# Huber loss on one core: subtraction in pieces, one load queue, a fourth output buffer, and a hand-ordered end

## The chip, the cores and the metric

The kernel runs on one core of a Trainium2 chip. The metric is device time in microseconds (us), the median of the executions. All runs told here were in the fast state, every kernel gave the right result, and the TensorE clock plays no part, as TensorE does nothing. Engine names in the profile: POOL is GpSimd, DVE is VectorE, ACT is ScalarE, SP is SyncE (it only issues loads here); a small q after a name (ACTq) is that engine's instruction sequencer.

## The reference

Two inputs of 8192 x 8192 in fp32, one output of the same shape in fp32:

```python
diff = pred - target
abs_diff = np.abs(diff)
return np.where(abs_diff <= 1.0, 0.5 * diff**2, abs_diff - 0.5)
```

That is 537 MB in, 268 MB out, and a handful of elementwise operations on 67 million elements. The kernel computes it as 0.5 * min(|d|, 1)^2 + max(|d| - 1, 0).

## The kernel before

The array is cut into 64 row tiles of 128 x 8192. Each tile is loaded in two halves of 4096 columns, each half as a pair of 2.10 MB loads. The differences are kept in bf16; the store converts back to fp32 on its way out.

```python
pool_a = ctx.enter_context(tc.tile_pool(name="sbuf_a", bufs=3))
pool_b = ctx.enter_context(tc.tile_pool(name="sbuf_b", bufs=3))
pool_d = ctx.enter_context(tc.tile_pool(name="sbuf_d", bufs=2))
pool_s = ctx.enter_context(tc.tile_pool(name="sbuf_s", bufs=3))
# ... emit_loads(i), for each half j of tile i:
nc.sync.dma_start(out=a, in_=pred_t[i, :, c0 : c0 + COLS])
beng = nc.sync if j == 0 else nc.scalar          # second halves on ScalarE's queue
beng.dma_start(out=b, in_=targ_t[i, :, c0 : c0 + COLS])
# ... do_tail, for the tile before:
nc.scalar.activation(out=s, in_=s, func=Act.Square, scale=SQRT_HALF)   # L68
nc.scalar.activation(out=d, in_=d, func=Act.Relu, bias=neg1.ap())      # L69
nc.vector.tensor_tensor(out=s, in0=s, in1=d, op=Alu.add)               # L70
# ... the loop:
for i in range(n_rt):
    emit_loads(i + 1)
    do_tail(0)
    for j in range(n_ct):
        nc.gpsimd.tensor_tensor(                                       # L85
            out=dfull[:, c0 : c0 + COLS], in0=a, in1=b, op=Alu.subtract)
    nc.scalar.activation(out=dfull, in_=dfull, func=Act.Abs)           # L90
    nc.vector.tensor_scalar(                                           # L91
        out=sfull, in0=dfull, scalar1=1.0, scalar2=None, op0=Alu.min)
    flush(1)                  # the store of an earlier tile, issued by GpSimd (L63)
    pending_tail.append((sfull, dfull, i))
```

A scheduler orders the instructions of each engine, so the order of the source is not always the order that runs.

Of the kernel before, what the change touches and what calls it, by code (L numbers as in the profile page):

```python
# [1 line left out]

# [4 lines left out]


@with_exitstack
def kernel(  # L10
    ctx: ExitStack,
    tc: tile.TileContext,
    pred: bass.AP,
    target: bass.AP,
    out: bass.AP,
):
    nc = tc.nc
    P = 128
    fp32 = mybir.dt.float32
    bf16 = mybir.dt.bfloat16  # L20
    Alu = mybir.AluOpType
    Act = mybir.ActivationFunctionType

    n_rows, n_cols = pred.shape
    COLS = 4096
    n_ct = n_cols // COLS
    SQRT_HALF = 0.70710678118654752

    pred_t = pred.rearrange("(n p) m -> n p m", p=P)
    targ_t = target.rearrange("(n p) m -> n p m", p=P)  # L30
    out_t = out.rearrange("(n p) m -> n p m", p=P)
    n_rt = pred_t.shape[0]

    neg1 = nc.alloc_sbuf_tensor("huber_neg1_bf16", [P, 1], bf16)
    nc.gpsimd.memset(neg1.ap(), -1.0)  # L35

    pool_a = ctx.enter_context(tc.tile_pool(name="sbuf_a", bufs=3))
    pool_b = ctx.enter_context(tc.tile_pool(name="sbuf_b", bufs=3))
    pool_d = ctx.enter_context(tc.tile_pool(name="sbuf_d", bufs=2))
    pool_s = ctx.enter_context(tc.tile_pool(name="sbuf_s", bufs=3))  # L40

    loads = {}
    pending_tail = []
    pending_store = []

    def emit_loads(i):
        if i >= n_rt:
            return
        tl = []
        for j in range(n_ct):  # L50
            c0 = j * COLS
            a = pool_a.tile([P, COLS], fp32)
            b = pool_b.tile([P, COLS], fp32)
            nc.sync.dma_start(out=a, in_=pred_t[i, :, c0 : c0 + COLS])  # L54
            beng = nc.sync if j == 0 else nc.scalar
            beng.dma_start(out=b, in_=targ_t[i, :, c0 : c0 + COLS])  # L56
            tl.append((a, b))
        loads[i] = tl

    def flush(limit):  # L60
        while len(pending_store) > limit:
            r, pi = pending_store.pop(0)
            nc.gpsimd.dma_start(out=out_t[pi, :, :], in_=r)  # L63

    def do_tail(limit):
        while len(pending_tail) > limit:
            s, d, pi = pending_tail.pop(0)
            nc.scalar.activation(out=s, in_=s, func=Act.Square, scale=SQRT_HALF)  # L68
            nc.scalar.activation(out=d, in_=d, func=Act.Relu, bias=neg1.ap())  # L69
            nc.vector.tensor_tensor(out=s, in0=s, in1=d, op=Alu.add)  # L70
            pending_store.append((s, pi))

    emit_loads(0)
    for i in range(n_rt):
        dfull = pool_d.tile([P, n_cols], bf16)
        sfull = pool_s.tile([P, n_cols], bf16)

        emit_loads(i + 1)

        do_tail(0)  # L80

        for j in range(n_ct):
            c0 = j * COLS
            a, b = loads[i][j]
            nc.gpsimd.tensor_tensor(  # L85
                out=dfull[:, c0 : c0 + COLS], in0=a, in1=b, op=Alu.subtract
            )
        del loads[i]

        nc.scalar.activation(out=dfull, in_=dfull, func=Act.Abs)  # L90
        nc.vector.tensor_scalar(  # L91
            out=sfull, in0=dfull, scalar1=1.0, scalar2=None, op0=Alu.min,
        )

        flush(1)

        pending_tail.append((sfull, dfull, i))

    do_tail(0)
    flush(0)  # L100


# [1 line left out]
_INS = ['pred', 'target']  # L104
_OUTS = [((8192, 8192), 'float32')]


# [23 lines left out]
```

## Time and profile before

| | before |
|---|---|
| median of four runs | 1942.36 us (1942.27 to 1942.46) |
| span of the profiled run | 1940.8 us |
| bytes moved | 805.4 MB, 415 GB/s on average |
| one tile in the steady part | 29.63 us |

The costliest groups of the page of the kernel before. Columns: line, engine, operation, output and input, shapes, count; then the busy us and the mean ns of one; then the idle us just before them and what ended most of it.

```profile
L85 POOL TENSOR_TENSOR dfull<-a,b 128x4096 bf16<-128x4096 f32 x128 | 1253.1, 9804 | 607.1 <-issue 577.8
L68 ACT ACTIVATE sfull<-sfull 128x8192 bf16<-128x8192 bf16 x64 | 449.9, 7030 | 543.9 <-DVE sfull L91 543.9
L70 DVE TENSOR_TENSOR sfull<-sfull,dfull 128x8192 bf16<-128x8192 bf16 x64 | 283.2, 4426 | 903.0 <-ACT dfull L69 903.0
L91 DVE TENSOR_SCALAR sfull<-dfull 128x8192 bf16<-128x8192 bf16 x64 | 539.6, 8432 | 199.9 <-ACT dfull L90 199.9
```

To see: the min (L91) costs more than the add (L70), though it reads one input instead of two, and ScalarE's Square (L68) loses 543.9 us waiting for it. GpSimd's idle time is put down to "issue", so no wait that the profile shows ended it; the prediction works out from the timeline what it really waits for.

### The profile page before, as it was taken

What the parts mean: (1) busy time and instruction counts of PE and PEld (TensorE: products, weight loads), DVE (VectorE), ACT (ScalarE), POOL (GpSimd) and SP (SyncE); (2) the same over time, 40 slices, a digit from 0 to 9 for tenths busy, and PEclk for the clock granted to TensorE, in tenths of its full rate; (3) what the DMA queues carried; (4) which work ended last, traced back from release to release, by engine and by line L of the source; (5) the groups of instructions that cost most, each with busy time, mean ns of one, the idle gap of its engine ahead of it and who ended that gap; (6) DMA issues with size and microseconds to landing.
All of it is one profiled execution on the core that took longest, in us unless ns stands there. A gap on an engine that the chain in (4) does not pass through costs nothing.

```text
span 1940.8 us, 1386 instructions
## 1 busy us (share of the span) xinstructions
DVE 822.9 (42%) x128; ACT 1343.0 (69%) x193; POOL 1286.6 (66%) x197
## 2 busy tenths in 40 slices
DVE  0345344354353453443543534534434435345342
ACT  2866867767668668677677686686676776866865
POOL 5676676676766766866767667668667676676680
DMA  9999999999999999999999999999999999999966
GB/s 404 376 420 428 421 427 426 425 424 424 424 428 422 426 424 424 425 425 423 426 426 423 427 424 424 422 429 423 424 425 426 425 424 424 424 424 424 426 274 260
DMA packets 46091, 805.42 MB, mean 415 GB/s; under 512 B 5120, under 2 KB 5120, under 8 KB 5120
## 3 DMA queue, kind: packets, MB, share of 16 engines
q1 hardware_dynamic: 27648, 402.67, 53.5%
q0 software_dynamic: 9216, 268.44, 32.5%
q10 hardware_dynamic: 9216, 134.22, 16.2%
q14 instruction: 11, 0.09, 0.0%
HBM read 536.87 MB, written 268.44 MB: 415 GB/s over the span
## 4 chain that ended last, share of the span: by engine, by line
ACT 50%; DVE 27%; issue 20%; POOL 1%; DMA 1%; POOLq 0%; SPq 0%; ACTq 0%
DVE sfull L91 27%; ACT dfull L90 22%; ACT sfull L68 22%; ACT dfull L69 6%; POOL dfull L85 1%; DMA b<-in_target_dram 1%; POOL out_dram L63 0%; POOLq L126 0%; SPq L54 0%; ACTq L56 0%; POOLq L85 0%; POOLq L63 0%
## 5 line engine op out<-in xcount | busy, mean ns | idle before, releaser
L85 POOL TENSOR_TENSOR dfull<-a,b 128x4096 bf16<-128x4096 f32 x128 | 1253.1, 9804 | 607.1 <-issue 577.8
L68 ACT ACTIVATE sfull<-sfull 128x8192 bf16<-128x8192 bf16 x64 | 449.9, 7030 | 543.9 <-DVE sfull L91 543.9
L70 DVE TENSOR_TENSOR sfull<-sfull,dfull 128x8192 bf16<-128x8192 bf16 x64 | 283.2, 4426 | 903.0 <-ACT dfull L69 903.0
L91 DVE TENSOR_SCALAR sfull<-dfull 128x8192 bf16<-128x8192 bf16 x64 | 539.6, 8432 | 199.9 <-ACT dfull L90 199.9
L90 ACT ACTIVATE dfull<-dfull 128x8192 bf16<-128x8192 bf16 x64 | 448.8, 7013 | 33.2 <-POOL dfull L85 33.2
L69 ACT ACTIVATE dfull<-dfull,huber_neg_bf 128x8192 bf16<-128x8192 bf16 x64 | 454.8, 7106 | 0.0
L63 POOL DMA_DIRECT2D out_dram<-sfull x64 | 36.6, 572 | 32.4 <-DVE sfull L70 32.4
L90 ACT ACT_TABLE_LOAD x1 | 1.3, 1283 | 1.2 <-PEq L115 1.2
L35 POOL MEMSET huber_neg_bf<- 128x1 bf16 x1 | 0.1, 101 | 0.3 <-POOLq L115 0.3
L115 POOL MEMSET const-float32-0.0<- 128x1 f32 x1 | 0.1, 98 | 0.2 <-issue 0.2
L115 POOL MEMSET const-bfloat16-1.0<- 128x1 bf16 x1 | 0.1, 101 | 0.0
L115 POOL MEMSET const-uint8-127<- 128x1 uint8 x1 | 0.1, 101 | 0.0
L115 POOL MEMSET const-float32-1.0<- 128x1 f32 x1 | 0.1, 98 | 0.0
## 6 DMA issues: line engine op xcount, KB each, us to landing
a<-in_pred_dram SPq DMA_DIRECT2D x128, 2048.0 KB, 18.0
out_dram<-sfull POOLq DMA_DIRECT2D x64, 4096.0 KB, 20.0
b<-in_target_dram ACTq DMA_DIRECT2D x64, 2048.0 KB, 13.8
b<-in_target_dram SPq DMA_DIRECT2D x64, 2048.0 KB, 24.6
```

What stands on the lines that cost most here:

```text
L35: nc.gpsimd.memset(neg1.ap(), -1.0)
L63: nc.gpsimd.dma_start(out=out_t[pi, :, :], in_=r)
L68: nc.scalar.activation(out=s, in_=s, func=Act.Square, scale=SQRT_HALF)
L69: nc.scalar.activation(out=d, in_=d, func=Act.Relu, bias=neg1.ap())
L70: nc.vector.tensor_tensor(out=s, in0=s, in1=d, op=Alu.add)
L85: nc.gpsimd.tensor_tensor(out=dfull[:, c0 : c0 + COLS], in0=a, in1=b, op=Alu.subtract)
L90: nc.scalar.activation(out=dfull, in_=dfull, func=Act.Abs)
L91: nc.vector.tensor_scalar(out=sfull, in0=dfull, scalar1=1.0, scalar2=None, op0=Alu.min,)
L115: nc = _bacc.Bacc("TRN2", target_bir_lowering=False, num_devices=1)
```

## The change

The intent is to let VectorE's min get in between shorter subtractions, to keep the loads in one queue that never runs dry, and to draw the last two tiles apart so that they do not pass the whole chain one after the other. There are four parts: four output buffers instead of three; all target loads on the sync queue; each half subtracted in two pieces of 2048 columns, with GpSimd's order fixed by hand; and the last two tiles written out by hand in small pieces, VectorE taking part of the work of ScalarE and GpSimd.

```diff
-    pool_s = ctx.enter_context(tc.tile_pool(name="sbuf_s", bufs=3))
+    pool_s = ctx.enter_context(tc.tile_pool(name="sbuf_s", bufs=4))
-            beng = nc.sync if j == 0 else nc.scalar
+            beng = nc.sync
-    for i in range(n_rt):
+    with tc.manual_schedule(engines={mybir.EngineType.Pool}):
+        for i in range(n_rt - 2):
 ... (loads, tail and the rest of the body as before)
-            nc.gpsimd.tensor_tensor(
-                out=dfull[:, c0 : c0 + COLS], in0=a, in1=b, op=Alu.subtract
-            )
+                for h0 in range(0, COLS, COLS // 2):
+                    h1 = h0 + COLS // 2
+                    nc.gpsimd.tensor_tensor(
+                        out=dfull[:, c0 + h0 : c0 + h1],
+                        in0=a[:, h0:h1], in1=b[:, h0:h1], op=Alu.subtract)
 ... (the end; orders of POOL, DVE and ACT fixed by hand)
+    flush(2)  # the store of tile 59
+    with tc.manual_schedule(engines=order):
+        asq(s61); arelu(d61)                    # tile 61's tail
+        ...                                     # tile 62: two subtractions on GpSimd
+        flush(1)  # the store of tile 60
+        vclamp(s_h1, d_h1); vstt(s_h1, d_h1); vmul(s_h1, d_h1)   # 62, half 1: VectorE alone
+        st62h1()
+        vadd(s61, d61)
+        flush(0)  # the store of tile 61
+        aabs(d_h0); vmin(s_h0, d_h0); asq(s_h0); arelu(d_h0)     # 62, half 0
+        sub63(V, 0); sub63(V, 1); sub63(V, 2)                    # 63: subtracted by VectorE
+        vadd(s_h0, d_h0); st62h0()
+        sub63(V, 3)
+        ... # 63: quarters 0 and 2 by Abs/min/Square/Relu/add, 1 and 3 by VectorE alone;
+        ... # four stores of one quarter each
```

(Several statements are put on one line here, and small helpers are left out: vclamp, vstt and vmul compute c = clamp(d, -1, 1), then c * (d - c/2), which is the same function without ScalarE.)

More of the change, by code (lines that the diff above doesn't have):

```diff
@@ L71, in do_tail, with act_path @@
             pending_store.append((s, pi))
-    emit_loads(0)
-    for i in range(n_rt):
-        dfull = pool_d.tile([P, n_cols], bf16)
-        sfull = pool_s.tile([P, n_cols], bf16)
-        emit_loads(i + 1)
-        do_tail(0)
+    def act_path(d, s):
+        nc.scalar.activation(out=d, in_=d, func=Act.Abs)
+        nc.vector.tensor_scalar(
+            out=s, in0=d, scalar1=1.0, scalar2=None, op0=Alu.min
+        )
+        nc.scalar.activation(out=s, in_=s, func=Act.Square, scale=SQRT_HALF)
+        nc.scalar.activation(out=d, in_=d, func=Act.Relu, bias=neg1.ap())
+        nc.vector.tensor_tensor(out=s, in0=s, in1=d, op=Alu.add)
@@ new lines, in dve_path @@
+    def dve_path(d, s):
+        nc.vector.tensor_scalar(
+            out=s, in0=d, scalar1=-1.0, scalar2=1.0, op0=Alu.max, op1=Alu.min
+        )
+        nc.vector.scalar_tensor_tensor(
+            out=d, in0=s, scalar=-0.5, in1=d, op0=Alu.mult, op1=Alu.add
+        )
+        nc.vector.tensor_tensor(out=s, in0=s, in1=d, op=Alu.mult)
+    emit_loads(0)
+    with tc.manual_schedule(engines={mybir.EngineType.Pool}):
+        for i in range(n_rt - 2):
+            dfull = pool_d.tile([P, n_cols], bf16)
+            sfull = pool_s.tile([P, n_cols], bf16)
+            emit_loads(i + 1)
+            do_tail(0)
+            for j in range(n_ct):
+                c0 = j * COLS
+                a, b = loads[i][j]
+                for h0 in range(0, COLS, COLS // 2):
+                    h1 = h0 + COLS // 2
+                    nc.gpsimd.tensor_tensor(
+                        out=dfull[:, c0 + h0 : c0 + h1],
+                        in0=a[:, h0:h1],
+                        in1=b[:, h0:h1],
+                        op=Alu.subtract,
+                    )
+            del loads[i]
+            nc.scalar.activation(out=dfull, in_=dfull, func=Act.Abs)
+            nc.vector.tensor_scalar(
+                out=sfull, in0=dfull, scalar1=1.0, scalar2=None, op0=Alu.min,
+            )
+            flush(1)
+            pending_tail.append((sfull, dfull, i))
@@ new lines, with vmin, vclamp @@
+    i62 = n_rt - 2
+    i63 = n_rt - 1
+    H = n_cols // 2
+    d62 = pool_d.tile([P, n_cols], bf16, tag="dfull")
+    s62 = pool_s.tile([P, n_cols], bf16, tag="sfull")
+    emit_loads(i63)
+    (s61, d61, _i61) = pending_tail.pop(0)
+    pending_store.append((s61, _i61))
+    V, A, G = nc.vector, nc.scalar, nc.gpsimd
+    def vmin(s, d):
+        V.tensor_scalar(out=s, in0=d, scalar1=1.0, scalar2=None, op0=Alu.min)
+    def vclamp(s, d):
+        V.tensor_scalar(
+            out=s, in0=d, scalar1=-1.0, scalar2=1.0, op0=Alu.max, op1=Alu.min
+        )
@@ new lines, in vstt, with vmul, vadd, aabs @@
+    def vstt(s, d):
+        V.scalar_tensor_tensor(
+            out=d, in0=s, scalar=-0.5, in1=d, op0=Alu.mult, op1=Alu.add
+        )
+    def vmul(s, d):
+        V.tensor_tensor(out=s, in0=s, in1=d, op=Alu.mult)
+    def vadd(s, d):
+        V.tensor_tensor(out=s, in0=s, in1=d, op=Alu.add)
+    def aabs(d):
+        A.activation(out=d, in_=d, func=Act.Abs)
+    def asq(s):
+        A.activation(out=s, in_=s, func=Act.Square, scale=SQRT_HALF)
+    def arelu(d):
+        A.activation(out=d, in_=d, func=Act.Relu, bias=neg1.ap())
@@ L82 @@
+    bounds = [0, 2048, 4096, 6144, 8192]
+    order = {mybir.EngineType.Pool, mybir.EngineType.DVE, mybir.EngineType.Activation}
+    flush(2)
+    with tc.manual_schedule(engines=order):
+        asq(s61)
+        arelu(d61)
         for j in range(n_ct):
-            c0 = j * COLS
-            a, b = loads[i][j]
-            nc.gpsimd.tensor_tensor(
-                out=dfull[:, c0 : c0 + COLS], in0=a, in1=b, op=Alu.subtract
-            )
-        del loads[i]
-        nc.scalar.activation(out=dfull, in_=dfull, func=Act.Abs)
@@ L91 @@
-        nc.vector.tensor_scalar(
-            out=sfull, in0=dfull, scalar1=1.0, scalar2=None, op0=Alu.min,
-        )
-        flush(1)
-        pending_tail.append((sfull, dfull, i))
-    do_tail(0)
-    flush(0)
+            a, b = loads[i62][j]
+            G.tensor_tensor(
+                out=d62[:, j * COLS : (j + 1) * COLS], in0=a, in1=b, op=Alu.subtract
+            )
+        flush(1)
+        d_h0, s_h0 = d62[:, 0:H], s62[:, 0:H]
+        d_h1, s_h1 = d62[:, H:n_cols], s62[:, H:n_cols]
@@ new lines, with sub63, D, S @@
+        d63 = s63 = None
+        def sub63(eng, k):
+            lo, hi = bounds[k], bounds[k + 1]
+            a, b = loads[i63][lo // COLS]
+            o0, o1 = lo % COLS, (hi - 1) % COLS + 1
+            eng.tensor_tensor(
+                out=d63[:, lo:hi], in0=a[:, o0:o1], in1=b[:, o0:o1], op=Alu.subtract
+            )
+        def D(k):
+            return d63[:, bounds[k] : bounds[k + 1]]
+        def S(k):
+            return s63[:, bounds[k] : bounds[k + 1]]
+        def st(k):
+            G.dma_start(out=out_t[i63, :, bounds[k] : bounds[k + 1]], in_=S(k))
@@ new lines, in st62h0, with st62h1 @@
+        def st62h0():
+            G.dma_start(out=out_t[i62, :, 0:H], in_=s_h0)
+        def st62h1():
+            G.dma_start(out=out_t[i62, :, H:n_cols], in_=s_h1)
+        vclamp(s_h1, d_h1)
+        vstt(s_h1, d_h1)
+        vmul(s_h1, d_h1)
+        st62h1()
+        vadd(s61, d61)
+        flush(0)
+        d63 = pool_d.tile([P, n_cols], bf16, tag="dfull")
+        s63 = pool_s.tile([P, n_cols], bf16, tag="sfull")
+        aabs(d_h0)
+        vmin(s_h0, d_h0)
+        asq(s_h0)
+        arelu(d_h0)
@@ new lines @@
+        sub63(V, 0)
+        sub63(V, 1)
+        sub63(V, 2)
+        vadd(s_h0, d_h0)
+        st62h0()
+        sub63(V, 3)
+        aabs(D(0))
+        aabs(D(2))
+        vmin(S(0), D(0))
+        vmin(S(2), D(2))
+        asq(S(0))
+        arelu(D(0))
+        vclamp(S(1), D(1))
+        vstt(S(1), D(1))
+        vmul(S(1), D(1))
+        st(1)
+        vadd(S(0), D(0))
+        st(0)
+        asq(S(2))
+        arelu(D(2))
+        vclamp(S(3), D(3))
+        vstt(S(3), D(3))
+        vmul(S(3), D(3))
@@ L104 @@
+        st(3)
+        vadd(S(2), D(2))
+        st(2)
 _INS = ['pred', 'target']
```

## The prediction

> **What bounds the kernel now.** I read the page first: engine shares, the row of GB/s in 40 slices, the chain that ended last; then the timeline of one period late in the run, the stretches table where I suspected the transfers, and last the timeline of the end. Tiles are numbered 0 to 63; a tile has a first and a second half of 4096 columns, each a pair of 2.10 MB loads.
>
> The page has no engine near full, but the transfers are (columns: 40 slices; then queue, packets, MB, share):
>
> ```profile
> DVE 822.9 (42%) x128; ACT 1343.0 (69%) x193; POOL 1286.6 (66%) x197
> GB/s 404 376 420 428 421 427 426 425 424 424 424 428 422 426 424 424 425 425 423 426 426 423 427 424 424 422 429 423 424 425 426 425 424 424 424 424 424 426 274 260
> q1 hardware_dynamic: 27648, 402.67, 53.5%
> q0 software_dynamic: 9216, 268.44, 32.5%
> ```
>
> To see: three stretches, a start under 424, a long plateau at 424, two slices at 274 and 260. If 424 is the ceiling of the transfers, only the ends can be won. It looks like the ceiling; the timeline of one period says it is not what sets the pace (columns: start, length, engine, line, output and input, idle before and releaser):
>
> ```profile
> 1742.71 7.11 ACT L69 ACTIVATE dfull<-dfull,huber_neg_bf 128x8192 bf16<-128x8192 bf16 x1
> ...
> 1749.85 4.43 DVE L70 TENSOR_TENSOR sfull<-sfull,dfull 128x8192 bf16<-128x8192 bf16 x1 [14.11 <-ACT dfull L69]
> 1754.42 19.64 POOL L85 TENSOR_TENSOR dfull<-a,b 128x4096 bf16<-128x4096 f32 x2 [9.48 <-issue]
> 1756.77 8.60 DVE L91 TENSOR_SCALAR sfull<-dfull 128x8192 bf16<-128x8192 bf16 x1 [2.50 <-ACT dfull L90]
> 1763.25 0.33 SPq L54 DMA_DIRECT2D a<-in_pred_dram  x1
> ...
> 1765.41 7.03 ACT L68 ACTIVATE sfull<-sfull 128x8192 bf16<-128x8192 bf16 x1 [8.67 <-DVE sfull L91]
> 1772.34 7.11 ACT L69 ACTIVATE dfull<-dfull,huber_neg_bf 128x8192 bf16<-128x8192 bf16 x1
> ```
>
> To see: POOL's subtraction starts at 1754.42, 0.14 after the add ends (1754.28), though its idle time is booked as "issue": it waits for the add to free the difference buffer (two buffers), not for data. Its first half ends at 1763.25 (the load into the freed buffer is issued then), and the min, ready at 1756.77, ends at 1765.37, 2.1 after that. From one Relu to the next: 4.43 add, 0.14, 8.83 first subtraction, 2.12 rest of the min, 7.03 Square, 7.11 Relu, less 0.03 net of overlaps and hand-overs: 29.63 us, and the Relus are 29.63 apart (1742.71, 1772.34). This loop sets the pace. A tile moves 4 x 2.10 + 4.19 = 12.58 MB, and 12.58 over 29.63 is the plateau's 424.6.
>
> Do the transfers have anything left? Columns: stretch, busy by engine, clock, DMA share, GB/s:
>
> ```profile
> 4.00:36.00 32.00, 0.00 (x0) 0.29 (x1) 17.88 (x3) 1.00 1.01 431
> 72.00:76.00 4.00, 4.00 (x1) 0.00 (x0) 4.00 (x2) 1.00 0.28 66
> 1746.00:1750.00 4.00, 0.15 (x1) 4.00 (x2) 0.00 (x0) 1.00 1.03 406
> 1750.00:1774.00 24.00, 12.88 (x2) 15.33 (x3) 19.58 (x2) 1.00 1.06 429
> 1876.00:1894.00 18.00, 7.91 (x1) 10.06 (x2) 17.11 (x3) 1.00 0.07 29
> 1914.00:1928.00 14.00, 4.43 (x1) 7.30 (x2) 0.53 (x1) 1.00 0.09 37
> ```
>
> To see: 431 with loads alone, 429 in 24 us of a period, and a dip to 406 around 1746 to 1750, just after a store and new loads were issued at 1744.4: the queues had run nearly dry, as the next loads are issued only when the loop frees a buffer. So the loop is slower than the transfers by about one percent. The other lines are holes: 4 us near the start, 18 and 14 us at the end, where tiles 62 and 63 pass the whole chain one after the other:
>
> ```profile
> 1904.93 2.29 DVE L91 TENSOR_SCALAR sfull<-dfull 128x8192 bf16<-128x8192 bf16 x1 [2.50 <-ACT dfull L90]
> ...
> 1921.34 4.43 DVE L70 TENSOR_TENSOR sfull<-sfull,dfull 128x8192 bf16<-128x8192 bf16 x1 [14.11 <-ACT dfull L69]
> 1926.06 0.53 POOL L63 DMA_DIRECT2D out_dram<-sfull  x1 [22.78 <-DVE sfull L70]
> ```
>
> To see: the same min takes 2.29 when POOL is idle; the last store is issued at 1926.06 and the span ends 14.7 later (9.7 of transfer, 5 of start and completion).
>
> **What the Trainium skill says.** "SBUF — State Buffer", section "Who interferes with whom": a VectorE op in a 2-port mode and a GpSimd op exclude each other for a whole instruction, and tensor_scalar can be in such a mode. The trace agrees: 8.60 beside a subtraction, ending 2.1 after it, 2.29 alone. "DMA: Bandwidth & Descriptors", section "Specifications": fabric ceiling 435 GB/s; the trace reaches 431. The same page, "Queues, rings and completion order": each DMA engine takes turns between queues, one packet each. The page's packets average 29 KB in q0 (stores) and 14.6 KB in q1 (loads), so a store beside q1 alone should take two thirds. "VectorE: DVE Perf Modes", "The perf-mode tier table": an fp32 tensor_tensor of 2048 columns takes 2293 ns; no row here shows it, and I use it for the subtractions that move to VectorE.
>
> **The change part by part.**
>
> 1. POOL's subtraction in two pieces per half (tiles 0 to 61). 8.83 / 2 gives about 4.42 a piece (estimate). POOL starts 4.57 after Relu's end, its first piece ends at 9.0, and the min, ready at 7.0, ends at 11.1 instead of 15.5. The loop becomes 29.63 - 4.4 = 25.2 us. That is shorter than the 12.58 MB can be moved, so the transfers take over. At 430 GB/s (between 429 and 431) a tile takes 29.26 us: 0.37 a tile, not 4.4.
>
> 2. All target loads on the sync queue; four output buffers. Neither is a wait now (the min waits only for Abs, the subtraction only for the add). They keep loads in order and off ScalarE's instruction stream, and give stores more time. 0 us by themselves; one load queue instead of two leaves stores the larger share.
>
> 3. Does the load queue stay full once transfers bind? At the end E of a tile's subtraction three pairs are reserved: one nearly landed, one queued, one just issued, beside a 4.19 MB store. The store takes about 14.6 us at two thirds of 430, loads get 2.1 MB meanwhile, then all. The first of the next tile's pairs is there by E + 2.5, the second at E + 20.3, its subtraction ends at E + 29.2. One or two pairs are always queued: no dip.
>
> 4. Time of E for tile 61. By then loads up to pair 124 are in but 0.36 MB, and stores 0 to 58: 125 x 4.194 - 0.36 + 59 x 4.194 = 771.4 MB, at 430 GB/s 1794.0 us. Lost at the start: 2.3 (first latency), 0.7 (a dip at 36 to 44), and the hole at 72 to 76. This grows: pair 7 is issued when tile 2's first half is subtracted, now with the min between the pieces, at 76.4 instead of 74.1, so 6.9 instead of about 4.5. E = 1794.0 + 9.9 = 1803.9. Before, it is 1833.3: 29.4 us won, of which some 8 because the faster loop first runs ahead until the queues are full, the rest the 0.37 a tile.
>
> 5. The end, from E = 0. Tile 62's second subtraction ends at 29.1 (part 3; ScalarE's Relu of tile 61 at about 29.5). VectorE: clamp 1.2, scalar_tensor_tensor 4.4 (estimate, one column per cycle), multiply 2.3: store of half of 62 at 37; add of 61, store at 41.6. Meanwhile the store of tile 60 (from 30.8) and those behind it hold two thirds of the bandwidth, and the last pair, with 3.9 MB to go, lands only at about 58. Then VectorE, in order: subtraction 2.3, add 2.3, store of 62's other half at 63; subtraction 2.3, two mins 1.4, clamp, scalar_tensor_tensor and multiply 4.2, add 1.2, the same 5.4 again: last store at 77. With 2.4 for its 1.05 MB and the 5 above: 85. Before, the same stretch is 1940.8 - 1833.3 = 107.5. Won: 22.5.
>
> Sum: 1803.9 + 85 = 1889 us of span, and the measured time is 1.6 above the span: 1890 us. Cross-check: 805.4 MB at 430 is 1873; plus 9.9 at the start and about 8 of gaps at the end gives 1891.
>
> **Rivals.**
>
> - The transfers have nothing left: 424.6 is the ceiling with loads and stores mixed. For: 35 slices say so. Against: the 406 dip inside each period, and the loop that adds up without them. Then E = 771.4 / 0.4246 + 9.9 = 1826.7, end 1912, time 1913: 1.5% less, within 2%.
> - VectorE does not get the ports between two pieces of a half, or ends up behind POOL again at the add, and the loop stays at 29.6. Against: the min did run between the two halves. Only the end is won: about 1920.
> - The end is better than drawn: if the last pair lands earlier, all that bounds is 805.4 MB at 431 plus start and completion, 1880. If VectorE's chain of small instructions or its hold on the ports delays the stores, 1900.
> - The late landing of the last pair costs more than the end wins: it would take 20 us more of VectorE's waiting than drawn; nothing suggests it.
>
> **Range and chances.** 1890, 8 in 10 between 1876 and 1915. The limit of 2% is at 1903.5. The first two rivals, together about 23%, fall within 2%; a bad end adds little. Faster 0.76, same 0.23, slower 0.01.
>
> **What would show it.** Plateau at 429 to 431 instead of 424; POOL's waits put down to loads and no longer to "issue"; the min shorter than 8.6; tile 61's subtraction ending near 1804; the last pair landing near 58 after that with a VectorE wait; no slice under 300 in the end but the last. Wrong if the plateau stays at 424 to 425 or ScalarE still waits 8.7 for each min with POOL never waiting for loads.

## The result, and the profile after

| | before | after |
|---|---|---|
| median | 1942.35 us (12 runs, 1942.19 to 1942.63) | 1886.26 us (8 runs, 1886.09 to 1886.38) |
| span of the profiled run | 1940.8 us | 1884.5 us |
| one tile in the steady part | 29.63 us | 29.24 us |
| mean of the GB/s slices of the steady part | 424.6 (slices 3 to 38) | 430.8 (slices 3 to 39) |
| E: end of tile 61's subtraction | 1833.3 us | 1802.2 us |
| from E to the end of the span | 107.5 us | 82.3 us |

The ratio of after to before is 0.971 (95% interval 0.970 to 0.972). Ratios here and below are the mean time of one kernel's fast runs over the mean of the other's fast runs of the same rounds, so not quite the ratio of the medians quoted.

The page of the kernel after: the same parts as the prediction showed of before.

```profile
DVE 766.9 (41%) x143; ACT 1329.2 (71%) x196; POOL 1294.3 (69%) x323
GB/s 410 381 432 430 433 429 430 432 430 435 427 430 432 429 434 429 430 432 430 431 430 432 432 429 431 435 427 432 429 431 435 426 434 429 429 432 430 432 431 367
q1 hardware_dynamic: 36864, 536.89, 70.9%
q0 software_dynamic: 9792, 268.44, 33.5%
...
L106 POOL TENSOR_TENSOR dfull<-a,b 128x2048 bf16<-128x2048 f32 x248 | 1239.8, 5017 | 531.1 <-DMA b<-in_target_dram 287.2
L70 DVE TENSOR_TENSOR sfull<-sfull,dfull 128x8192 bf16<-128x8192 bf16 x61 | 476.0, 7803 | 860.7 <-ACT dfull L69 860.7
...
L68 ACT ACTIVATE sfull<-sfull 128x8192 bf16<-128x8192 bf16 x61 | 428.8, 7030 | 250.5 <-DVE sfull L115 250.5
...
L115 DVE TENSOR_SCALAR sfull<-dfull 128x8192 bf16<-128x8192 bf16 x62 | 254.7, 4108 | 226.2 <-ACT dfull L114 226.2
```

To see: the plateau is 430 and lasts to the slice before the last. GpSimd's idle time now ends mostly with a load ("DMA b"), no longer with "issue". The min (L115 now) has halved, from 8432 to 4108 ns, and ScalarE's wait for it with it. No engine is near full; the transfers are the bound. The add has grown from 4426 to 7803 ns, and it costs nothing, as the period below shows.

Timeline of the kernel after, early in the run, before the load queue has filled up. Columns: start, length, engine, line, operation, output and input, count, and in brackets the idle time before and what ended it.

```profile
83.07 7.01 ACT L114 ACTIVATE dfull<-dfull 128x8192 bf16<-128x8192 bf16 x1
...
87.77 19.95 POOL L106 TENSOR_TENSOR dfull<-a,b 128x2048 bf16<-128x2048 f32 x4 [4.73 <-issue]
90.12 4.30 DVE L115 TENSOR_SCALAR sfull<-dfull 128x8192 bf16<-128x8192 bf16 x1 [2.50 <-ACT dfull L114]
...
108.40 7.01 ACT L114 ACTIVATE dfull<-dfull 128x8192 bf16<-128x8192 bf16 x1
```

To see: this is the loop on its own, with data always at hand. One Abs to the next is 25.33 us instead of 29.63, and the min takes 4.30 instead of 8.60.

Timeline of the kernel after, one period of the steady part:

```profile
1705.52 8.96 POOL L106 TENSOR_TENSOR dfull<-a,b 128x2048 bf16<-128x2048 f32 x2 [4.81 <-DMA b<-in_target_dram]
1710.45 8.31 DVE L70 TENSOR_TENSOR sfull<-sfull,dfull 128x8192 bf16<-128x8192 bf16 x1 [14.11 <-ACT dfull L69]
1714.43 0.57 POOL L63 DMA_DIRECT2D out_dram<-sfull  x1
...
1714.52 7.03 ACT L114 ACTIVATE dfull<-dfull 128x8192 bf16<-128x8192 bf16 x1 [4.10 <-POOL dfull L106]
...
1718.91 11.01 POOL L106 TENSOR_TENSOR dfull<-a,b 128x2048 bf16<-128x2048 f32 x2 [3.91 <-DVE sfull L70]
1721.58 3.98 DVE L115 TENSOR_SCALAR sfull<-dfull 128x8192 bf16<-128x8192 bf16 x1 [2.81 <-ACT dfull L114]
...
1743.67 0.57 POOL L63 DMA_DIRECT2D out_dram<-sfull  x1
```

To see: from one store issue to the next is 29.24 us. The second-half subtraction (1705.52) starts when its load lands, after 4.81 us of idleness. The add (1710.45) now falls beside that subtraction and ends 4.3 us after it, as if it had waited for it. The next subtraction does wait 3.91 us for the add, but 29.24 us later GpSimd stands idle for a load again, so that delay is slack.

### The profile page after: what moved, and what is told of

Its sections match the earlier page's. It is cut to its first block, busy times and chain, and to the rows that moved or that the text cites. A ratio compares the mean times of both kernels' runs of the same rounds, so it can differ in the third digit from the quotient of the medians.

```text
span 1884.5 us, 1407 instructions
## 1 busy us (share of the span) xinstructions
DVE 766.9 (41%) x143; ACT 1329.2 (71%) x196; POOL 1294.3 (69%) x323
## 3 DMA queue, kind: packets, MB, share of 16 engines
q0 software_dynamic: 9792, 268.44, 33.5%
HBM read 536.87 MB, written 268.44 MB: 427 GB/s over the span
## 4 chain that ended last, share of the span: by engine, by line
DMA 35%; ACT 26%; POOL 21%; DVE 13%; issue 3%; SPq 0%; POOLq 0%
DMA b<-in_target_dram 35%; POOL dfull L106 21%; ACT sfull L68 9%; ACT dfull L114 9%; ACT dfull L69 8%; DVE sfull L70 8%; DVE sfull L115 5%; SPq L54 0%; POOL out_dram L63 0%; POOL out_dram L196 0%; POOLq L106 0%; POOLq L268 0%; POOL out_dram L202 0%; POOL out_dram L199 0%; POOL d L173 0%
## 5 line engine op out<-in xcount | busy, mean ns | idle before, releaser
L106 POOL TENSOR_TENSOR dfull<-a,b 128x2048 bf16<-128x2048 f32 x248 | 1239.8, 5017 | 531.1 <-DMA b<-in_target_dram 287.2
L70 DVE TENSOR_TENSOR sfull<-sfull,dfull 128x8192 bf16<-128x8192 bf16 x61 | 476.0, 7803 | 860.7 <-ACT dfull L69 860.7
L114 ACT ACTIVATE dfull<-dfull 128x8192 bf16<-128x8192 bf16 x62 | 435.8, 7029 | 264.8 <-POOL dfull L106 264.8
L68 ACT ACTIVATE sfull<-sfull 128x8192 bf16<-128x8192 bf16 x61 | 428.8, 7030 | 250.5 <-DVE sfull L115 250.5
L69 ACT ACTIVATE dfull<-dfull,huber_neg_bf 128x8192 bf16<-128x8192 bf16 x61 | 433.5, 7106 | 0.0
L115 DVE TENSOR_SCALAR sfull<-dfull 128x8192 bf16<-128x8192 bf16 x62 | 254.7, 4108 | 226.2 <-ACT dfull L114 226.2
L173 POOL TENSOR_TENSOR d<-a,b 128x4096 bf16<-128x4096 f32 x2 | 17.6, 8818 | 10.9 <-DMA b<-in_target_dram 7.0
L159 ACT ACTIVATE sfull<-sfull 128x8192 bf16<-128x8192 bf16 x1 | 7.0, 7030 | 8.4 <-DVE sfull L115 8.4
L185 DVE TENSOR_TENSOR d<-a,b 128x2048 bf16<-128x2048 f32 x4 | 9.1, 2286 | 7.3 <-DMA b<-in_target_dram 7.3
L145 DVE SCALAR_TENSOR_TENSOR d<-s,d 128x2048 bf16<-128x2048 bf16 (+1 forms) x3 | 9.0, 3003 | 0.1
L162 ACT ACTIVATE dfull<-dfull,huber_neg_bf 128x8192 bf16<-128x8192 bf16 x1 | 7.1, 7107 | 0.0
L150 DVE TENSOR_TENSOR s<-s,d 128x2048 bf16<-128x2048 bf16 (+1 forms) x3 | 4.7, 1580 | 0.1
L153 DVE TENSOR_TENSOR s<-s,d 128x2048 bf16<-128x2048 bf16 (+1 forms) x3 | 4.7, 1572 | 0.0
L153 DVE TENSOR_TENSOR sfull<-sfull,dfull 128x8192 bf16<-128x8192 bf16 x1 | 4.4, 4418 | 0.0
## 6 DMA issues: line engine op xcount, KB each, us to landing
out_dram<-sfull POOLq DMA_DIRECT2D x62, 4096.0 KB, 18.8
```

The costliest lines, as they stand in the source:

```text
L106: nc.gpsimd.tensor_tensor(out=dfull[:, c0 + h0 : c0 + h1], in0=a[:, h0:h1], in1=b[:, h0:h1], op=Alu.subtract,)
L115: nc.vector.tensor_scalar(out=sfull, in0=dfull, scalar1=1.0, scalar2=None, op0=Alu.min,)
L153: V.tensor_tensor(out=s, in0=s, in1=d, op=Alu.add)
L159: A.activation(out=s, in_=s, func=Act.Square, scale=SQRT_HALF)
L162: A.activation(out=d, in_=d, func=Act.Relu, bias=neg1.ap())
L173: G.tensor_tensor(out=d62[:, j * COLS : (j + 1) * COLS], in0=a, in1=b, op=Alu.subtract)
```

## The experiments

split_only, uneven, end_only and queue_buffer were put on record first, to take the change apart; the others followed from what these showed. They are told here by subject.

**split_only.** The kernel before with the pieces alone.

```diff
-            nc.gpsimd.tensor_tensor(out=dfull[:, c0 : c0 + COLS], in0=a, in1=b, ...)
+            for h0 in range(0, COLS, COLS // 2):      # two pieces of 2048
+                nc.gpsimd.tensor_tensor(out=dfull[:, c0 + h0 : c0 + h1], in0=a[:, h0:h1], ...)
```

> The kernel before with one thing of the change: each half of the subtraction on GpSimd in two equal pieces, for all 64 tiles. Theory (the min's wait for the port set the pace): the min falls from 8.6 to about 4.3 us, the plateau goes from 424 to about 430 GB/s, a tile takes 29.2 us instead of 29.63, and subtractions wait for loads. Tile 61 subtracted at about 1803 instead of 1833; the old end of 107 us unchanged: about 1911 us. Rival (the single load queue or the fourth output buffer made the plateau faster): plateau stays at 424, about 1942 us.

Measured: 1969.23 us, ratio 1.014 (1.012 to 1.015). It is slower than the kernel before, and the expectation was missed by 58 us. The timeline of split_only, half of one period:

```profile
1029.71 15.46 POOL L87 TENSOR_TENSOR dfull<-a,b 128x2048 bf16<-128x2048 f32 x3 [9.70 <-issue]
1032.06 4.30 DVE L96 TENSOR_SCALAR sfull<-dfull 128x8192 bf16<-128x8192 bf16 x1 [2.50 <-ACT dfull L95]
...
1040.73 0.36 ACTq L56 DMA_DIRECT2D b<-in_target_dram  x1
1041.20 7.03 ACT L68 ACTIVATE sfull<-sfull 128x8192 bf16<-128x8192 bf16 x1 [9.17 <-POOL dfull L87]
```

To see: the min did become short (4.30, ended at 1036.36). Yet Square starts only at 1041.20. Ahead of it in ScalarE's stream stands the issue of a target load, which may go only when the first half's buffer has been subtracted, at 1040.73. ScalarE's 9.17 us of idleness is put down to GpSimd, not to the min. In the kernel before, the same issue was hidden:

```profile
1763.25 0.36 ACTq L56 DMA_DIRECT2D b<-in_target_dram  x1
```

To see: it goes at 1763.25, and the min ends only at 1765.37 (the lines are in the prediction). So the pieces won 4.3 us on the min and the load issue took more than that back: the wait that took the place of the removed one was an instruction that I had not counted as work.

**two_queues.** The same from the other side: the kernel after with its second-half target loads back on ScalarE's queue.

```diff
-            beng = nc.sync
+            beng = nc.sync if j == 0 else nc.scalar
```

> The changed kernel with the target loads of the second halves on ScalarE's queue again, as before the change. Theory: ScalarE's stream stops at each such load until the first half of the next tile has been subtracted, the Square waits for GpSimd and not for the min, a tile takes about 30.1 us as in the run with the pieces alone, the plateau falls to about 416 GB/s; about 1935 to 1945 us. Rival (once transfers bind, the queue does not matter): 1886 within 0.5%.

Measured: 1943.01 us, ratio 1.000 (0.999 to 1.001). The entire gain is gone, the new end notwithstanding. The view of waits of two_queues (engine, what it works on, what it waited for; us in total, times, longest):

```profile
ACT sfull L68 <- POOL dfull L106: 550.5, 60, 9.5
```

To see: 60 waits of Square for GpSimd, in nearly every tile, as in split_only (61 there). The load issue in ScalarE's stream is the cause in both, since moving it is the only edit here.

**end_only.** The kernel after with whole halves instead of pieces; queue, buffers and end stay.

```diff
-                for h0 in range(0, COLS, COLS // 2):
-                    h1 = h0 + COLS // 2
+                for h0 in range(0, COLS, COLS):
+                    h1 = h0 + COLS
```

> The changed kernel with the subtractions of tiles 0 to 61 in one piece per half again; new end, single load queue and four output buffers stay. Theory: the plateau goes back to 424 GB/s and 29.63 us a tile, tile 61 subtracted at about 1830; the end takes less than the 82 us of the changed kernel, about 71 to 75, because the load queue is not full when it begins and the last pair lands earlier: about 1905 us. So the two parts do not add up: 31 and 37 alone, 56 together. Rival (the parts add): 1942 less 56 plus 31, 1917 us.

Measured: 1908.41 us, ratio 0.9825 (0.981 to 0.984), so 34 us. E is at 1830.4 here, about as before, and the end after E lasts 76.1 us. In the kernel after, the same end takes 82.3.

**queue_buffer.** The kernel before with all loads on the sync queue and four output buffers.

```diff
-    pool_s = ctx.enter_context(tc.tile_pool(name="sbuf_s", bufs=3))
+    pool_s = ctx.enter_context(tc.tile_pool(name="sbuf_s", bufs=4))
-            beng = nc.sync if j == 0 else nc.scalar
+            beng = nc.sync
```

> The kernel before with all loads on the sync queue and four output buffers, nothing else. Theory: the loop through the min sets the pace, so the plateau stays at 424; only the first pair lands earlier (near 13 instead of 18 us), worth 0 to 4 us: 1938 to 1942 us. Rival (mixing two load queues cost bandwidth): plateau up to 430, about 1912 us.

Measured: 2531.14 us, ratio 1.303 (1.301 to 1.305), a miss by nearly 600 us. Timeline of queue_buffer, half of one period:

```profile
1036.94 4.42 DVE L70 TENSOR_TENSOR sfull<-sfull,dfull 128x8192 bf16<-128x8192 bf16 x1 [14.11 <-ACT dfull L69]
1041.66 0.57 POOL L63 DMA_DIRECT2D out_dram<-sfull  x1 [20.99 <-DVE sfull L70]
1042.25 17.58 POOL L85 TENSOR_TENSOR dfull<-a,b 128x4096 bf16<-128x4096 f32 x2
1043.86 18.13 DVE L91 TENSOR_SCALAR sfull<-dfull 128x8192 bf16<-128x8192 bf16 x1 [2.49 <-ACT dfull L90]
```

To see: the scheduler moved the store. It now stands between the add and the next two subtractions, and waits for that add itself (20.99 us). The min takes 18.13 us: it ends 2.2 us after the second subtraction and not, as before, after the first. A tile takes 39.16 us. Built without the fourth buffer, the one queue alone gives GpSimd the same sequence of instructions; the fourth buffer alone leaves it as before. That is read from the built kernels, neither of which was run. Why the min waits for both subtractions here is not shown (see join).

**ordered.** queue_buffer once more, with GpSimd's order fixed to that of the source.

```diff
-    for i in range(n_rt):
+    with tc.manual_schedule(engines={mybir.EngineType.Pool}):
+        for i in range(n_rt):
```

> The kernel before with the single load queue, four output buffers and GpSimd's own order kept as written (subtractions, then the store): the run with one queue and four buffers, 2531 us, plus this order. Theory now: what cost 589 us there was that the scheduler put the store between the add and the next subtractions, so that the min waited for both halves (17.7 us); with the store behind the subtractions the min is back at 8.6 us, the tile at 29.63 us, the plateau at 424, and the time at 1938 to 1942 us. Rival (the single queue or the buffers are slow in themselves): stays above 2000 us.

Measured: 1940.01 us, ratio 0.9988 (0.998 to 0.9995). The min is back at 8447 ns. So the 600 us of queue_buffer are the order of GpSimd's instructions, and the queue and the buffer by themselves, in a good order, are worth 0.1%.

**split_sync3.** The kernel before with the pieces, the one queue and the fixed order, but three output buffers and the old end (the edits of split_only and ordered, less the buffer line).

> The kernel before with the two pieces per half, all loads on the sync queue and GpSimd's order kept; three output buffers and the old end stay. Theory: ScalarE's own load issues, which stood in front of the Square and waited for a buffer, cost the pieces alone their gain (1969 us); without them the min is near 4.2 us, subtractions wait for loads, the plateau is 430 GB/s, and with the old end the time is about 1911 us (1905 to 1918). Rival (the fourth output buffer is needed too): plateau under 426 and the time over 1925.

Measured: 1905.47 us, ratio 0.981 (0.979 to 0.983). Lines of its page:

```profile
GB/s 408 386 431 428 435 431 427 431 431 430 433 429 433 430 429 433 428 431 434 428 431 432 429 433 429 431 433 429 432 433 426 434 428 431 431 429 431 435 357 265
...
L88 POOL TENSOR_TENSOR dfull<-a,b 128x2048 bf16<-128x2048 f32 x256 | 1279.8, 5017 | 548.6 <-DMA b<-in_target_dram 296.9
```

To see: the full plateau, with three output buffers, and the old end's last slices (357, 265). GpSimd waits for loads as in the kernel after. E is at 1802.4, within 0.2 us of the kernel after. So the fourth buffer gives the loop nothing, and the loop's part of the gain is the pieces together with the queue: 64 us apart from split_only, which differs from this by the queue and the fixed order. That the queue is needed is shown by two_queues, which has the order; whether the pieces with the one queue need the fixed order was not run.

**uneven.** Is it the number of pieces that helps the min, or where the first one ends? The kernel before with each half in two pieces, cut at 768 and not at 2048 (diff cut to its main line).

```diff
+                for h0, h1 in ((0, 768), (768, COLS)):
```

> The kernel before with each half of the subtraction in two pieces of 768 and 3328 columns. Theory: the first piece ends about 6.3 us after the Relu, before the min is ready at 7.0, so the min still waits for the end of the second piece at about 13.4; the min stays near 8.6 us, the pace at 29.6 us, the plateau at 424: 1942 us, within 0.3%. Rival (more and smaller pieces help in themselves, or let the VectorE in more often): the min falls by some us and the time falls towards that of the equal pieces, 1911 to 1925 us.

Measured: 1952.09 us, ratio 1.005 (1.0035 to 1.0065). Timeline of uneven:

```profile
1048.44 19.93 POOL L86 TENSOR_TENSOR dfull<-a,b 128x768 bf16<-128x768 f32 x4 [9.33 <-issue]
1050.80 8.75 DVE L95 TENSOR_SCALAR sfull<-dfull 128x8192 bf16<-128x8192 bf16 x1 [2.50 <-ACT dfull L94]
```

To see: the min is ready 2.4 us after the subtractions begin, when the short first piece is already over by proportion (768/4096 of 8.83 is 1.7 us, an estimate). It then waits for the long second piece and takes 8.75 us, no less than before. So the number of pieces does not help; the piece that runs at the moment the min is ready has to be short. The loss of 0.5%, which I had not expected, goes with what pieces cost: GpSimd is busy 1271.9 us here and 1253.1 before, 18.8 us for 128 further instructions, 0.15 us each. One further piece per tile lies ahead of the min's end, in the loop that sets the pace: half of the 18.8 is 9.4 us, and the kernel lost 9.7 (an account by sums; no run isolates it).

**quarter.** The kernel after with pieces of 1024 (edit: COLS // 4 in place of COLS // 2).

> The changed kernel with four pieces of 1024 columns per half instead of two of 2048. Theory: the min waits less still, but the transfers bind, so the plateau stays at 430 to 431 and the time at 1886 within 0.5%. Rival (the min's wait is still what sets the pace): another 1% or more gained, 1867 or less; or the extra pieces' cost shows as a loss of 0.5% or more.

Measured: 1886.02 us (1884.90 to 1887.09), ratio 0.971 (0.969 to 0.9725), the same as the kernel after. But the expectation that the min waits less still was missed. Line of its page:

```profile
L115 DVE TENSOR_SCALAR sfull<-dfull 128x8192 bf16<-128x8192 bf16 x62 | 284.6, 4590 | 388.8 <-ACT dfull L114 388.8
```

To see: the min takes 4590 ns, against 4108 in the kernel after. Early in the run one Abs follows the other after 25.47 us (81.18 to 106.65), against 25.33, so the loop is no faster with four pieces than with two. The run shows that cutting further brings nothing; it does not test what a faster loop would give.

**after_d3.** The kernel after with three difference buffers and three output buffers, which together need no more room.

```diff
-    pool_d = ctx.enter_context(tc.tile_pool(name="sbuf_d", bufs=2))
-    pool_s = ctx.enter_context(tc.tile_pool(name="sbuf_s", bufs=4))
+    pool_d = ctx.enter_context(tc.tile_pool(name="sbuf_d", bufs=3))
+    pool_s = ctx.enter_context(tc.tile_pool(name="sbuf_s", bufs=3))
```

> The changed kernel with three difference buffers and three output buffers instead of two and four. Theory: the third tile's subtraction no longer waits for the first add, so the next loads are issued about 12 us earlier and the hole near the start (second slice, 381 GB/s) closes; nothing else changes: about 5 us less, 1881 us. Rival (the store now waits for the add in front of the subtractions, and the min waits for several pieces as in the run at 2531 us): plateau below 430, time over 1890 us.

Measured: **1881.81 us** (1881.73 to 1881.84), ratio 0.969 (0.967 to 0.970): 4.45 us under the kernel after, and, with d3_late below, the fastest of all. Its page:

```profile
GB/s 407 429 432 430 432 436 425 434 428 430 432 430 432 429 430 433 429 433 428 430 435 427 433 428 432 435 425 433 432 429 431 430 432 434 427 435 426 432 432 361
```

To see: the second slice is 429, where the kernel after has 381. A slice is 47.1 us, so 48 GB/s in it are 5.3 us of transfer at 430. This is the hole at 72 to 76 that the prediction lists as a loss at the start. With two difference buffers the subtraction waits for the add, and no load can be issued meanwhile; with three the hole is gone: from 72 to 76 us the kernel after moves 119 GB/s, after_d3 438. (That the fourth output buffer isn't missed was seen in split_sync3.)

The next two asked what bounds the end.

**late_store.** The kernel after, with the store of tile 60 put behind the store of tile 62's second half, so that the last loads meet fewer stores. If VectorE's chain after the last landing binds, as the prediction had it, this should win; if the bytes left do, it should not.

```diff
-        flush(1)  # the store of tile 60
 ...
         st62h1()
+        flush(1)  # the store of tile 60
```

> The changed kernel with the store of tile 60 issued after that of the first half of tile 62, 8 us later. Theory: in the end a store holds two thirds of the bandwidth; without it the last pair of loads lands about 40 us after tile 61's subtraction instead of 54, VectorE does not wait for it, and the gaps of the last 15 us shrink: 2 to 4 us less, 1882 to 1884 us. Rival (the end is bound by the bytes left): within 1 us of 1886.

Measured: 1886.77 us, ratio 0.971 (0.970 to 0.973), no better, where 1882 to 1884 was expected. The timelines of the end, first of the kernel after, then of late_store:

```profile
1793.22 8.96 POOL L106 TENSOR_TENSOR dfull<-a,b 128x2048 bf16<-128x2048 f32 x2 [4.81 <-DMA b<-in_target_dram]
...
1822.44 8.83 POOL L173 TENSOR_TENSOR d<-a,b 128x4096 bf16<-128x4096 f32 x1 [7.04 <-DMA b<-in_target_dram]
...
1832.57 4.43 DVE L145 SCALAR_TENSOR_TENSOR d<-s,d 128x4096 bf16<-128x4096 bf16 x1
...
1844.71 4.49 DVE L185 TENSOR_TENSOR d<-a,b 128x2048 bf16<-128x2048 f32 x2
...
1856.54 2.29 DVE L185 TENSOR_TENSOR d<-a,b 128x2048 bf16<-128x2048 f32 x1 [7.35 <-DMA b<-in_target_dram]
...
1875.38 0.53 POOL L196 DMA_DIRECT2D out_dram<-s  x1 [0.60 <-DVE s L153]
```

```profile
1844.91 6.69 DVE L184 TENSOR_TENSOR d<-a,b 128x2048 bf16<-128x2048 f32 x3
...
1868.91 0.53 POOL L195 DMA_DIRECT2D out_dram<-s  x1 [0.60 <-DVE s L153]
```

To see: in the kernel after, VectorE waits 7.35 us for the last pair and subtracts from 1856.54. In late_store it goes through its third subtraction without a wait, and the last store is issued 6.5 us earlier; the kernel ends no earlier. The stretches of the two kernels say where the time went (columns: stretch, its length, busy us and instructions of DVE, ACT and POOL, clock, DMA share, GB/s), first the kernel after, then late_store:

```profile
1824.00:1844.00 20.00, 12.62 (x5) 11.14 (x3) 9.23 (x4) 1.00 1.09 435
...
1862.00:1877.00 15.00, 12.95 (x11) 7.50 (x4) 2.12 (x4) 1.00 0.89 351
1877.00:1884.50 7.50, 0.00 (x0) 0.00 (x0) 0.00 (x0) 1.00 0.47 177
```

```profile
1824.00:1844.00 20.00, 12.43 (x5) 11.36 (x3) 8.57 (x3) 1.00 0.91 386
...
1862.00:1877.00 15.00, 6.55 (x6) 2.90 (x2) 2.12 (x4) 1.00 1.04 412
1877.00:1884.50 7.50, 0.00 (x0) 0.00 (x0) 0.00 (x0) 1.00 0.43 163
```

To see: holding the store back left the transfers at 386 GB/s for 20 us, where the kernel after has 435, and the stretch before the end paid it back with 412 instead of 351. The same bytes were moved in the same time. So VectorE's chain is not what sets the end by itself. Neither is it free. Each of the two kernels has a hole in its transfers, first the kernel after, then late_store:

```profile
1867.00:1870.00 3.00, 2.97 (x4) 3.00 (x3) 0.53 (x1) 1.00 0.27 104
```

```profile
1838.00:1841.00 3.00, 3.00 (x2) 0.00 (x0) 1.10 (x2) 1.00 0.30 128
```

To see: in the kernel after the hole lies just before the first store of tile 63 (issued at 1868.93), which waits for the chain; in late_store it lies where the loads are done and the store that was held back is not yet issued (1840.38). Each holds some 2 us of transfer at 430 GB/s (an estimate: 3 x (1 - 104/430)). The edit moved the hole and did not close it. A kernel with neither hole was not run, so what the chain still costs is open.

**d3_late.** after_d3 and late_store together.

> Both: three difference and three output buffers, and the late store of tile 60. Theory: the start and the end are separate, the gains add: 1877 to 1880 us. Rival (with three output buffers the last tile waits for the late store to land): no better than the three difference buffers alone.

Measured: 1881.88 us, ratio 0.969 (0.9675 to 0.970), the same as after_d3 alone; the 1877 to 1880 that was expected was missed, as with late_store, whose result was not yet known. The reason that the rival gave is not seen: in the end of this run VectorE waits 0.28 us, no more, for a store to land. Again the edit gains nothing.

**join.** This was to settle why the min of queue_buffer waits for both subtractions: the store ahead of them, with a tiny memset between, for which the first subtraction waits. The edit is against ordered, not against queue_buffer.

```diff
             do_tail(0)
+            flush(0)
+            nc.gpsimd.memset(dfull[:, 0:1], 0.0)
 ...
-            flush(1)
```

> The store in front of the subtractions, as the scheduler had it in the run with one queue and four buffers (2531 us, min 17.7 us), with one 128x1 memset on GpSimd between the store and the first subtraction, which the subtraction waits for. Theory: [...]the min goes back to about 8.6 us, a tile takes 30 to 31 us, the time 1950 to 2030 us. Rival (the order alone, or that the min asks earlier, is the cause): the min stays near 17 us and the time near 2530 us or above.

Measured: 3009.84 us, ratio 1.55. The timeline of join:

```profile
1503.27 0.57 POOL L63 DMA_DIRECT2D out_dram<-sfull  x1 [28.22 <-DVE sfull L70]
...
1504.05 17.56 POOL L87 TENSOR_TENSOR dfull<-a,b 128x4096 bf16<-128x4096 f32 x2
1521.64 7.03 ACT L92 ACTIVATE dfull<-dfull 128x8192 bf16<-128x8192 bf16 x1 [23.12 <-POOL dfull L87]
1528.70 2.29 DVE L93 TENSOR_SCALAR sfull<-dfull 128x8192 bf16<-128x8192 bf16 x1 [25.73 <-ACT dfull L92]
```

To see: an error of design. The subtractions of a tile come after the store of the tile before, so subtraction, Abs and min now follow one another, and the min meets no subtraction at all (2.29 us). The run says nothing about the question, which stays open. The Trainium skill's "GPSIMD Engine Reference", section "Instruction dispatch", says that consecutive GpSimd instructions are no barrier between its cores; cores out of step after a store, the idea that this run was meant to test, would be a candidate, but no run here shows it.

Why are the two parts of the gain not additive? split_sync3 won 37 us with the old end, end_only 34 us with the old pace, together 71; the kernel after won 56. The ends show most of it. At the old pace the new end shortens the stretch after E from 107.5 us (before) to 76.1 (end_only), by 31.4. At the new pace it goes from 101.4 (split_sync3) to 82.3 (after), by 19.1: when the loop is held back by loads, more of them are still queued at E, and the last pair lands 54 us after E, in end_only about 34. That is 12.3 of the 15 us. Another 2.9 is counted twice: end_only has the one queue too, and its E is 2.9 us earlier than before's.

## Why the prediction was right or wrong

**Step 1, the loop, was right.** Predicted: 25.2 us for the loop on its own, then the transfers at 29.26 a tile. Seen: 25.33 early, then 29.24. The min ends 11.25 us after Relu in that early period; 11.1 was predicted.

**Step 2, queue and buffers at "0 us by themselves", is the step that failed in part.** The fourth buffer is 0 (split_sync3), and queue and buffer together on the old loop are 0.1% (ordered). But the step's reason, that neither "is a wait now", holds for the old loop alone. There the load issue in ScalarE's stream was hidden: the min ended 2.1 us after the same event. Once step 1 shortens the min, that issue becomes the wait, and step 1 without step 2 loses 1.4% (split_only) or the whole gain (two_queues). The prediction credited step 1 with a gain that belongs to both, and did not see that the queue in turn needs the fixed order (queue_buffer, with whole halves). The sum was not touched, as all the parts were present.

**Step 3, the queue stays full, was right.** The second pair was to be there 20.3 us after the end of the tile before. For tile 62 that is 1802.2 + 20.3 = 1822.5, and its subtraction starts at 1822.44, released by a load. The two thirds on which this rests hold too: in the packets of this trace, the store issued at 1714.43 moves from about 1718 to 1732 and has 0.60 to 0.74 of the bytes in each 2 us of it.

**Step 4, E at 1803.9, came out at 1802.2.** The GB/s slices up to E add up to 773 MB, against 771.4 predicted, and the plateau is 430.8 instead of 430. The loss at the start was over-sized: the first two slices fall short of 430.8 by what amounts to 7.7 us, where 9.9 was put down. The first pair landed earlier with one queue (the first subtraction starts at 13.08, before at 18.12), so pair 7 was issued at 73.5 and not at 76.4.

**Step 5, the end of 85 us, came out at 82.3, but its account, VectorE's chain as the bound, was not confirmed.** The estimates of instructions held: 4.43 us for the scalar_tensor_tensor, 2.29 for an fp32 subtraction on VectorE, in agreement with the table that the prediction took it from. The last pair was there at 54.3 instead of 58, the last store was issued at 73.2 instead of 77, and from there to the end took 9.1 instead of 7.4. But late_store shows that bringing this chain forward by 6.5 us gains nothing, so the sum of its instructions is not by itself the bound. The prediction's own cross-check fits the runs better: 805.4 less 773 MB leave 32.4 MB, 75.3 us at 430, and some 7 us for gaps and completion; how much of these the chain could still give back is open. Both gave nearly the same number here, since the chain and the bytes end close together; that the step's sum came near is in part luck.

**The rivals.** That 424.6 is the ceiling is refuted by the plateau at 430.8. That VectorE might end up behind GpSimd at the add did happen (7803 ns instead of 4426), but only where GpSimd was waiting for loads anyway, so its consequence did not follow. Of the signs named in advance all were there: the plateau, the waits for loads, the shorter min, E near 1804, and the late last pair with a VectorE wait. Of the slices in the end only the last is low, and at 367 it isn't under 300 either.

The total: 31.1 us won up to E and 25.2 after it, where 29.4 and 22.5 were predicted.

## What to carry to other kernels

When a change shortens a wait, look for what else ends at nearly the same time in the waiting engine's stream, load issues included: an issue that waits for a buffer holds up the compute instructions behind it, and it shows only once the longer wait is gone. A GpSimd instruction that VectorE has to share ports with should be short at the moment VectorE becomes ready; more and shorter pieces help only there, and pieces of 1024 instead of 2048 brought nothing more. At the end of a kernel bound by transfers, count the bytes left before ordering instructions by hand, and see whether an edit closes a hole in the transfers or only moves it.

## What the Trainium skill lacked or had wrong

- "DMA: Bandwidth & Descriptors", section "Issuing engines are not separate DMA queues", says that issuing from several engines saves only sequencer time. It gives no figure for the opposite kind of cost: a load issue that waits for its buffer stalls the compute stream it stands in. ScalarE stood idle 9.2 us on average before 61 of the 64 Squares of split_only; with those issues on ScalarE the changed kernel takes 1943 us, without them 1886.
- "SBUF — State Buffer", section "Who interferes with whom", says that the loser blocks for a whole instruction, which agrees with 8.60 and 4.30 us for a min of 2.29. It also says that the instruction issued first gets the ports. That does not tell why, with a store issued right ahead of two subtractions, a min that was ready 1.6 us after the first of them started waited for the second as well (18.13 us). No run here settles it.
- "DMA: Bandwidth & Descriptors", section "Bandwidth", has 425 GB/s as the highest figure in its table of measurements, for loads alone. Loads and converting stores together kept 430.8 GB/s for over 1700 us here, on one core. The two are not quite alike: the profile counts a store by the fp32 bytes that it writes (268.44 MB), twice what its bf16 tiles hold.
- No page that I read has the cost of cutting a GpSimd operation into pieces: 0.15 us for each further instruction (18.8 us for 128).
